# Projections: second and fourth output change places from group to group, and the narrow groups' weight sums go to VectorE

## The chip, the cores and the metric

The kernel runs on one core of one Trainium2 chip. A core has five engines that run side by side, each with its own queue of instructions, taken in order: TensorE (PE in the profile; its weight loads are PEld), VectorE (DVE), ScalarE (ACT), GpSimd (POOL) and SyncE (SP), which here issues the DMA transfers. They hand work to each other by semaphores. The metric is the time of one execution in microseconds (us), as the median of several runs.

## The reference

One decoder layer over 2048 tokens of width 1024, in float32: a normed input, one combined projection, two mixers (gated linear attention and dilated sliding-window attention), an output projection and an MLP. The change touches only the combined projection:

```python
nx = rmsnorm(h, attn_norm_g[l])
proj = jnp.einsum('bsd,dp->bsp', nx, w_in[l])
gq, gk, gv, gr, glow, dq, dk_, dv_ = jnp.split(proj, split_at, axis=-1)
```

`gq`, `gk` are 256 columns each, `gv`, `gr`, `dq`, `dk_`, `dv_` 512 each, and `glow`, the low-rank input of the forget gate, 16.

## The kernel before

The projection is a matrix product of tokens (2048 x 1024) by weights (1024 x columns). It is done in two halves of 1024 tokens, and the columns in nine groups (L169): `dv`, `gr`, `dq`, `dk`, `dq`, `dk`, `gq`, `gk`, `gv`. So there are 18 groups `g`. Six are wide (a pair of 256 or 264 columns), twelve are narrow (`dq`, `dk`, `gq`, `gk`: a pair of 128 columns).

Each group is a 2 x 2 block product: two blocks of 512 tokens, two halves of the 1024 inputs, two blocks of columns. It is done with seven block products instead of eight, by sums of blocks ahead of and behind the products. A group therefore runs the products in the order 1, 2, 5, 6, 3, 4, 7 (L173), one job each. TensorE computes each float32 product as three products of a high and a low part (`mm3`, L63 to L66). A narrow job is 12 matmuls of 512 columns: four chunks of 128 inputs, three matmuls each.

**Weights.** The four blocks a11, a12, a21, a22 of a group lie in two buffers (`wraw`). `prep` (L196) makes ready one job's weights: ACT copies the block, scaled, into a rounded high part (L206), and DVE subtracts to get the low part (L208; L210 where there is a scale). The results go to one of three buffers (`wcomb`), two jobs ahead of the product. Between the jobs, blocks are summed in place: at job 2 a21 += a22 (L213), at job 5 a21 -= a11 (L215) and a12 -= a21 (L217), at job 6 a21 = a22 - a21 (L219). L211 chooses the engine of these sums: DVE in a wide group, GpSimd in a narrow one. As soon as a block is no longer needed, the same block of the next group is loaded over it: a11 after the sum at job 5, a12 behind job 3, a22 behind job 4, a21 behind job 7 (L215 and the lines behind it; L189 is the transfer, on SP's queue). The next group's sum at job 2 needs that last load.

**Outputs.** `product` (L280) computes a job into one of four PSUM banks in turn (tags a, c, a, o), and its `rest` (L298) takes it into the output buffers. There are six of these in SBUF: X, c11, c12, c21, c22 and `last`. Product 1 is copied to X (ACT, L307); product 2 plus X is the first output (DVE, L309); product 5 is copied to the fourth (ACT, L312); product 6 is added to X (L314), and X plus the fourth gives the start of the second (L315, DVE); product 3 completes the second (L317); product 4 is copied to the third (L320); product 7 is added to X (L322), and X to the third and the fourth (L323, L324). First, second, third and fourth output are always c11, c12, c21 and c22.

**Stores.** `finish` (L240) stores an output when it is complete: the first after product 2, the second after product 3, the fourth and the third after product 7. In a `dq` or `dk` group ACT and DVE first split it into a high and a low part in place (L252, L253), and SP stores both (L254, to qD or kD). In a `gq` or `gk` group it is stored as it is (L248). A buffer can be written by the next group once its store has read it. In a `gr` group the output passes through a sigmoid on ACT and DVE (L127 to L130, L264, L265) and a product on GpSimd (L266), and the 16 columns of `glow` go to `gate` (L227 to L238), whose small matmuls (L232, L235) and copies (L230, L233) run among those of the next groups.

**Order.** The first pieces of work are ordered by hand. Then a loop over jobs emits `prep(at + 2)`, `product(at)` and, in some places, a step of other work: the second token half's norm (L95, L96, L424, L426), its transposes (L374) and their copies and sums (L430 to L439). The order in which each engine runs all that is set by a scheduler with its own estimate of times, so an edit can move instructions that it doesn't name.

Of the kernel before, what the change touches and what calls it, by code (L numbers as in the profile page):

```python
# [14 lines left out]
OP = mybir.AluOpType  # L15
# [23 lines left out]
def emit(tc, a, stop=99):  # L39
    nc = tc.nc  # L40
    V, A, G, T, SP = nc.vector, nc.scalar, nc.gpsimd, nc.tensor, nc.sync
# [6 lines left out]
    def ps(tag):  # L48
        return psum.tile([128, 512], F32, name="ps_" + tag, tag=tag, bufs=BANKS[tag])
# [5 lines left out]
    def view(t, shape):  # L55
        n = int(np.prod(shape))
        names = "abcd"[:len(shape)]
        return t[:, :n].rearrange(f"p ({' '.join(names)}) -> p {' '.join(names)}", **dict(zip(names, shape)))
# [9 lines left out]
    def token_rows(ap, c, row, width=D):  # L68

        return bass.AP(tensor=ap.tensor, offset=ap.offset + c * 128 * row,  # L70
                       ap=[[row, 16], [16 * row, 8], [1, width]])
# [54 lines left out]
    def log_sigmoid(e, p):  # L126
        A.activation(e, p, AF.Abs)  # L127
        A.activation(e, e, AF.Exp, scale=-1.0)
        A.activation(e, e, AF.Ln, bias=1.0)
        V.scalar_tensor_tensor(e, p, 0.0, e, op0=OP.min, op1=OP.subtract)  # L130
# [27 lines left out]
    GP = 1056  # L158
    xp, bp, acc = slot("xp"), slot("bp"), [slot("acc") for _ in range(3)]
    CX, c11, c12, c21, c22, last = [t[:, GP * q:GP * q + GP] for t in acc for q in range(2)]  # L160
    C = [[c11, c12], [c21, c22]]
    stg_ring = view(last, (4, 264))
    stg_at = [0]

    def stage():
        stg_at[0] = (stg_at[0] + 1) % 4
        return stg_ring[:, stg_at[0]]
# [17 lines left out]
    def load_w(g, n, k):  # L185

        if g < 2 * NG:
            _, c0, w = groups[g % NG]
            SP.dma_start(raws[n][:, k, :, :w], w_in[:, 4 * k:4 * k + 4, c0 + n * w:c0 + n * w + w])  # L189

    def comb(at, w):

        t = view(combs[at % 3], (2, 4, max(w, 256)))
        return [t[:, q, :, :w] for q in range(2)]

    def prep(at):  # L196

        if at >= len(jobs):
            return
        g, j = jobs[at]  # L200
        kind, _, w = groups[g % NG]
        (a11, a12), (a21, a22) = [[raws[n][:, k, :, :w] for k in range(2)] for n in range(2)]
        hi, lo = comb(at, w)
        src = {1: a11, 2: a12, 5: a21, 6: a21, 3: a12, 4: a22, 7: a21}[j]
        sc = scales.get(kind, 1.0)
        A.activation(hi, src, AF.Copy, scale=sc)  # L206
        if sc == 1.0:
            V.tensor_tensor(lo, src, hi.bitcast(F32), op=OP.subtract)  # L208
        else:
            V.scalar_tensor_tensor(lo, src, sc, hi.bitcast(F32), op0=OP.mult, op1=OP.subtract)  # L210
        Y = V if w > 128 else G  # L211
        if j == 2 and g:
            Y.tensor_tensor(a21, a21, a22, op=OP.add)  # L213
        if j == 5:
            Y.tensor_tensor(a21, a21, a11, op=OP.subtract)  # L215
            load_w(g + 1, 0, 0)
            Y.tensor_tensor(a12, a12, a21, op=OP.subtract)  # L217
        if j == 6:
            Y.tensor_tensor(a21, a22, a21, op=OP.subtract)  # L219
        if j == 3:  # L220
            load_w(g + 1, 0, 1)
        if j == 4:
            load_w(g + 1, 1, 1)
        if j == 7:
            load_w(g + 1, 1, 0)

    def gate(glow, t):  # L227

        gT = gTs[t % 2]
        V.memset(gT, 1.0)  # L230
        pt = ps("d")
        T.transpose(pt[:16, :128], glow, ident)  # L232
        V.tensor_copy(gT[:16], pt[:16, :128])  # L233
        pg = ps("d")[:, :256]
        T.matmul(pg, gT, w2b, start=True, stop=True)  # L235
        e = stage()[:, :256]
        log_sigmoid(e, pg)
        SP.dma_start(glD[t * 128:t * 128 + 128], e)  # L238

    def finish(g, n, k, i):  # L240

        kind, c0, w = groups[g % NG]
        tb = 2 * (g // NG) + k
        c = C[n][k]
        if w == 128:
            tk = slice(512 * tb, 512 * tb + 512)
            if kind in ("gq", "gk"):
                SP.dma_start((gqD if kind == "gq" else gkD)[n, :, tk], c[:, :512])  # L248
                return
            pr = (c0 - (DQ if kind == "dq" else DK)) // 128 + n  # L250
            hi = c[:, 512:1024].bitcast(FR)
            A.activation(hi, c[:, :512], AF.Copy)  # L252
            V.tensor_tensor(c[:, :512], c[:, :512], hi.bitcast(F32), op=OP.subtract)  # L253
            SP.dma_start((qD if kind == "dq" else kD)[pr][:, :, tk], view(c, (2, 512)))  # L254
            return
        t = 4 * tb + i
        tk = slice(t * 128, t * 128 + 128)
        s = c[:, i * w:i * w + w]
        if kind == "gr":
            j = n * w  # L260
            m = min(w, 512 - j)
            sg = stage()[:, :m]
            log_sigmoid(sg, s[:, :m])
            A.activation(sg, sg, AF.Exp)  # L264
            V.tensor_tensor(s[:, :m], sg, s[:, :m], op=OP.mult)  # L265
            G.tensor_tensor(s[:, :m], s[:, :m], gnB[:, j:j + m], op=OP.mult)  # L266
            SP.dma_start(srD[tk, j:j + m], s[:, :m])
            if m < w:
                gate(s[:, m:w], t)
            return  # L270
        j = n * w
        if kind == "dv":
            SP.dma_start(token_rows(vN[:, j:], t, 512, w), s)
        if i == 3:
            SP.dma_start((vD if kind == "dv" else gvD)[512 * tb:512 * tb + 512, j:j + w].rearrange("(i p) n -> p i n", i=4),
                         c[:, :4 * w].rearrange("p (i n) -> p i n", i=4))
# [3 lines left out]
    def product(at, i):  # L280

        g, j = jobs[at]
        kind, _, w = groups[g % NG]
        p = ps("acao"[banks[0] % 4])
        banks[0] += 1
        B, W = TB[j], comb(at, w)
        n = w
        if w == 128:
            n = 512
            for c in range(4):  # L290
                mm3(p, W[0][:, c], W[1][:, c], B[0][:, c], B[1][:, c], c == 0, c == 3)
        else:
            p = p[:, :w]
            tk = slice(i * 128, i * 128 + 128)
            for c in range(4):
                mm3(p, B[0][:, c, tk], B[1][:, c, tk], W[0][:, c], W[1][:, c], c == 0, c == 3)

        def rest():  # L298
            X, c11, c12, c21, c22 = [v[:, i * n:i * n + n] for v in (CX, *C[0], *C[1])]
            q = p  # L300
            if kind == "dq":
                q, ix, i11, i12, i21, i22 = [v.rearrange(f"p (c {o}) -> p c r i", c=4, i=8) for v, o in
                                             ((p, "r i"), *((v, "i r") for v in (X, c11, c12, c21, c22)))]
            else:
                ix, i11, i12, i21, i22 = X, c11, c12, c21, c22
            if j == 1:
                A.activation(ix, q, AF.Copy)  # L307
            elif j == 2:
                V.tensor_tensor(i11, q, ix, op=OP.add)  # L309
                finish(g, 0, 0, i)  # L310
            elif j == 5:
                A.activation(i22, q, AF.Copy)  # L312
            elif j == 6:
                V.tensor_tensor(ix, q, ix, op=OP.add)  # L314
                V.tensor_tensor(c12, X, c22, op=OP.add)  # L315
            elif j == 3:
                V.tensor_tensor(i12, q, i12, op=OP.add)  # L317
                finish(g, 0, 1, i)
            elif j == 4:
                A.activation(i21, q, AF.Copy)  # L320
            else:
                V.tensor_tensor(ix, q, ix, op=OP.add)  # L322
                V.tensor_tensor(c21, c21, X, op=OP.add)  # L323
                V.tensor_tensor(c22, c22, X, op=OP.add)  # L324
                finish(g, 1, 1, i)
                finish(g, 1, 0, i)

        return rest
# [28 lines left out]
    X = {}  # L357
# [120 lines left out]
    with tc.manual_schedule(engines={nc.tensor.engine, nc.vector.engine, nc.scalar.engine, nc.gpsimd.engine}):  # L478
# [45 lines left out]
        a21, a22 = [raws[1][:, k, :, :256] for k in range(2)]  # L524
# [16 lines left out]
        kept(3, pv3)  # L541
        x_scale(5)
        prep(2)
        x_stat(6)
        first_half(4, pv4)
# [36 lines left out]
    for at in range(5, len(jobs)):  # L582
        g = jobs[at][0]
# [720 lines left out]

    def output(C, half, t, i, last=False):

        scr = sums["scr"][:, 512 * (i % 4):512 * (i % 4) + 512]
        ss = stat(2)
        for n in range(2):
            A.activation(scr, C[n], AF.Square, accum_out=ss[:, n:n + 1])  # L1310
            if n == 0:
                G.tensor_tensor(C[0], C[0], gF[:, :512], op=OP.mult)  # L1312
        s1 = stat()
        V.tensor_tensor(s1, ss[:, 0:1], ss[:, 1:2], op=OP.add)
        r = rstd_of(s1, D)
        V.scalar_tensor_tensor(C[1], C[1], r, gF[:, 512:], op0=OP.mult, op1=OP.mult)
        A.activation(C[0], C[0], AF.Copy, scale=r)
# [68 lines left out]
    for at in range(7, len(jobs1)):  # L1386
# [13 lines left out]
        if at in (len(jobs1) - 4, len(jobs1) - 2):  # L1400
            n = (at + 4 - len(jobs1)) // 2
# [5 lines left out]
    for ph, (j, half) in enumerate(phases):  # L1407
        P = [bank() for _ in range(4)]
        for k in range(8):
            n = 8 * ph + k  # L1410
# [74 lines left out]
```

## Time and profile before

| what | value |
|---|---|
| median of 3 runs | 2330.84 us (2328.76 to 2331.72) |
| the profiled execution | 2328.52 us |
| its span, first to last instruction | 2326.7 us |
| mean granted clock of TensorE | 0.995 of full speed |
| TensorE busy | 2286.6 us, 98% of the span |
| VectorE busy | 1571.9 us, 68% |
| ScalarE busy | 1146.3 us, 49% |
| GpSimd busy | 434.9 us, 19% |

In the rows of the profile a line such as L213 is a line of the kernel before. A row of a timeline has the start in us, the duration, the engine, the line, the operation, the tiles (output <- inputs), the shape, and in brackets how long the engine sat idle before and what ended that. A row of groups has the count, the busy time, the mean of one in ns, and the idle time before them with what ended it. The projections fill about the first 520 us of the span.

### The profile page before, as it was taken

How to read it: one execution, taken by the hardware profiler on the slowest of the kernel's cores; microseconds unless marked ns; L12 is line 12 of the kernel's file. 1: busy time of each engine (PE TensorE's matmuls, PEld its weight loads, DVE VectorE, ACT ScalarE, POOL GpSimd, SP SyncE). 2: the span in 40 equal slices, each digit the busy share in tenths (PEclk: the TensorE clock that was granted, in tenths of full speed). 3: DMA queues.
4: the chain of work that ended last, by engine and by line, in shares of the span. 5: the costliest groups of instructions: out<-in, count | busy, mean ns of one | idle time of the engine just before them, and what ended most of it. 6: DMA issues, size and time to landing. Idle time of an engine off the chain costs nothing.

```text
span 2326.7 us, 34991 instructions
## 1 busy us (share of the span) xinstructions
PE 2286.6 (98%) x12652; PEld 1974.4 (85%) x12652; DVE 1571.9 (68%) x2926; ACT 1146.3 (49%) x2200; POOL 434.9 (19%) x530
## 2 busy tenths in 40 slices
PE   8999999999999999999999999999999999999998
PEld 7977998789999998888888887888888888888886
DVE  8878778766676786446877788777765446447445
ACT  6565446535676773224555566555544323224324
POOL 1133103235387785000000000000000100001002
PEclk9999999999999999999999999999999999999999
DMA  4547754777666964778644447444486477447543
GB/s 158 152 153 246 227 178 123 214 226 244 196 218 209 296 194 158 221 233 269 209 155 152 157 155 261 165 150 150 149 276 236 162 271 262 139 160 270 202 162 109
DMA packets 341804, 457.59 MB, mean 197 GB/s; under 512 B 18117, under 2 KB 214230, under 8 KB 336256
## 3 DMA queue, kind: packets, MB, share of 16 engines
q1 hardware_dynamic: 336878, 446.71, 59.2%
q10 hardware_dynamic: 4754, 8.66, 1.0%
q8 instruction: 99, 1.62, 0.3%
q14 instruction: 73, 0.60, 0.1%
HBM read 292.99 MB, written 167.02 MB: 198 GB/s over the span
## 4 chain that ended last, share of the span: by engine, by line
PE 48%; DVE 2%; DMA 2%; issue 1%; ACT 0%; POOL 0%; POOLq 0%; DVEq 0%; ACTq 0%
PE ps_c L65 6%; PE ps_c L64 6%; PE ps_c L66 6%; PE ps_a L65 4%; PE ps_a L66 4%; PE ps_a L64 4%; PE ps_d L64 4%; PE ps_d L65 4%; PE ps_d L66 4%; PE ps_o L65 2%; PE ps_o L64 2%; PE ps_o L66 2%; DMA rb<-w_ff 1%; DMA rb<-hTD 0%; DVE cb L352 0%
## 5 line engine op out<-in xcount | busy, mean ns | idle before, releaser
L352 DVE TENSOR_TENSOR ca<-ra,ca 128x1024 fp32r<-128x1024 f32 x112 | 137.7, 1230 | 162.0 <-ACT ca L351 162.0
L1312 POOL TENSOR_TENSOR suma<-suma,gs 128x512 f32<-128x512 f32 x16 | 23.3, 1470 | 1146.6 <-ACT scr L1310 1146.5
L351 ACT ACTIVATE ca<-ra 128x1024 fp32r<-128x1024 f32 x112 | 117.9, 1053 | 223.6 <-PE ps_c L66 178.6
L351 ACT ACTIVATE w1comb<-w1raw 128x512 fp32r<-128x512 f32 x224 | 139.9, 627 | 155.3 <-PE ps_c L66 58.1
L352 DVE TENSOR_TENSOR w1comb<-w1raw,w1comb 128x512 fp32r<-128x512 f32 x224 | 154.0, 689 | 52.4 <-ACT w1comb L351 52.2
L716 ACT ACTIVATE pe<-pe,O 128x256 f32<-128x256 f32 (+1 forms) x384 | 155.7, 454 | 61.0 <-DVE O L715 59.0
L744 PE MATMUL ps_a<-v,pt 128*128 128x65 f32 x1200 | 178.3, 252 | 0.9 <-DVE pt L734 0.5
L744 PEld LDWEIGHTS ps_a<-v,pt 128*128 128x128 f32 x1200 | 175.3, 194 | 2.7 <-DVE pt L734 0.7
L725 PE MATMUL ps_d<-ident,pe 128*128 128x128 f32 x600 | 157.5, 278 | 3.2 <-ACT pt L732 3.0
L715 DVE CUSTOM_DVE_ANT_0 pe<-ps_c,nb 128x256 f32<-128x256 f32 (+1 forms) x384 | 125.8, 361 | 34.9 <-PE ps_d L725 15.9
L206 ACT ACTIVATE wcomb<-wraw 128x512 fp32r<-128x512 f32 (+2 forms) x126 | 96.6, 774 | 93.4 <-PE ps_o L65 22.2
L351 ACT ACTIVATE cb<-rb 128x1024 fp32r<-128x1024 f32 x56 | 59.4, 1061 | 162.1 <-PE ps_o L65 104.3
L65 PE MATMUL ps_c<-hb,w1comb 128*128 128x512 f32 x336 | 130.9, 390 | 0.6 <-DVE w1comb L352 0.6
L66 PE MATMUL ps_c<-hb,w1comb 128*128 128x512 f32 x336 | 130.8, 389 | 0.0
L64 PE MATMUL ps_c<-hb,w1comb 128*128 128x512 f32 x336 | 130.7, 389 | 0.0
L66 PE MATMUL ps_c<-cb,ca 128*128 128x512 f32 x336 | 130.7, 389 | 0.0
L64 PE MATMUL ps_c<-cb,ca 128*128 128x512 f32 x336 | 130.7, 389 | 0.0
L65 PE MATMUL ps_c<-cb,ca 128*128 128x512 f32 x336 | 130.7, 389 | 0.0
L725 PEld LDWEIGHTS ps_d<-ident,pe 128*128 128x128 f32 x600 | 107.7, 184 | 3.8 <-ACT pt L732 3.2
L208 DVE TENSOR_TENSOR wcomb<-wraw,wcomb 128x512 fp32r<-128x512 f32 (+2 forms) x84 | 89.8, 1070 | 28.8 <-ACT wcomb L206 28.2
L352 DVE TENSOR_TENSOR cb<-rb,cb 128x1024 fp32r<-128x1024 f32 x56 | 68.2, 1222 | 59.8 <-ACT cb L351 59.7
L1178 ACT ACTIVATE acc<-acc 128x512 f32<-128x512 f32 x128 | 79.6, 631 | 47.9 <-DVE acc L1198 35.9
(402 smaller groups left out, 7150.5 us busy)
## 6 DMA issues: line engine op xcount, KB each, us to landing
ra<-actD SPq DMA_DIRECT2D x56, 1024.0 KB, 6.9
actD<-acc SPq DMA_DIRECT2D x192, 256.0 KB, 2.4
rb<-w_ff SPq DMA_DIRECT2D x72, 512.0 KB, 4.5
w1raw<-w_ff SPq DMA_DIRECT2D x32, 1024.0 KB, 5.8
k<-kD SPq DMA_DIRECT2D x16, 1024.0 KB, 8.5
rb<-hTD SPq DMA_DIRECT2D x13, 1024.0 KB, 6.1
wraw<-w_in SPq DMA_DIRECT2D x48, 256.0 KB, 4.3
cmb<-boD SPq DMA_DIRECT2D x16, 528.0 KB, 6.4
```

Of the source, the lines that this page charges most:

```text
L64: T.matmul(out, sh, mh, start=first, stop=False)
L65: T.matmul(out, sl, mh, start=False, stop=False)
L66: T.matmul(out, sh, ml, start=False, stop=last)
L206: A.activation(hi, src, AF.Copy, scale=sc)
L208: V.tensor_tensor(lo, src, hi.bitcast(F32), op=OP.subtract)
L351: A.activation(hi, src, AF.Copy)
L352: V.tensor_tensor(lo, src, hi.bitcast(F32), op=OP.subtract)
L715: V.tensor_tensor_reduce(p, s, bias, scale=1.0, scalar=BIG, op0=OP.add, op1=OP.min, accum_out=nm)
L716: A.activation(p, p, AF.Exp, bias=nm, scale=-1.0)
L725: T.transpose(pb[:, i * 128:i * 128 + 128], src, ident)
L744: T.matmul(self.b.opsum[:, n % 4], self.pt[:, i * 128:i * 128 + 128], self.b.v[:, blk, cols], start=first, stop=last)
L1178: A.activation(v, v, AF.Relu)
```

## The change

Two edits. The first gives the second output and the fourth output of a group c12 and c22 by turns: in an even group as before, in an odd group the second is c22 and the fourth c12. So product 5's copy writes the buffer that held the previous group's second output, not its fourth. The second edit takes the choice of engine away: the sums of weights run on VectorE in the narrow groups too, 48 sums of 128 x 512. As the scheduler works anew, the order of instructions on all engines differs between about 103 and 300 us and again between about 370 and 490 us; elsewhere it is the same. The number of matmuls is the same.

```diff
-    C = [[c11, c12], [c21, c22]]
...
-        Y = V if w > 128 else G
         if j == 2 and g:
-            Y.tensor_tensor(a21, a21, a22, op=OP.add)
+            V.tensor_tensor(a21, a21, a22, op=OP.add)
         if j == 5:
-            Y.tensor_tensor(a21, a21, a11, op=OP.subtract)
+            V.tensor_tensor(a21, a21, a11, op=OP.subtract)
             load_w(g + 1, 0, 0)
-            Y.tensor_tensor(a12, a12, a21, op=OP.subtract)
+            V.tensor_tensor(a12, a12, a21, op=OP.subtract)
         if j == 6:
-            Y.tensor_tensor(a21, a22, a21, op=OP.subtract)
+            V.tensor_tensor(a21, a22, a21, op=OP.subtract)
...
+    def outputs(g):
+
+        return (c11, (c12, c22)[g % 2], c21, (c22, c12)[g % 2])
+
     def finish(g, n, k, i):
...
-        c = C[n][k]
+        c = outputs(g)[2 * n + k]
...
-            X, c11, c12, c21, c22 = [v[:, i * n:i * n + n] for v in (CX, *C[0], *C[1])]
+            X, c11, c12, c21, c22 = [v[:, i * n:i * n + n] for v in (CX, *outputs(g))]
```

## The prediction

> **What bounds the kernel now.** I read the page's busy table first, then the windows of 20 us, then TensorE's timeline where a window falls short of 20.
>
> ```profile
> PE 2286.6 (98%) x12652; PEld 1974.4 (85%) x12652; DVE 1571.9 (68%) x2926; ACT 1146.3 (49%) x2200; POOL 434.9 (19%) x530
> ```
>
> TensorE is the bound: 98% of the span. A change that keeps its 12,652 matmuls, as this one does, can only win where TensorE idles or is throttled. The rewritten lines run in two places, the narrow groups of the first token half (about 103 to 300 us) and of the second (370 to 490 us).
>
> ```profile
> 100.00:200.00 100.00, 94.19 (x465) 75.05 (x464) 81.56 (x138) 62.54 (x139) 38.05 (x30) 0.98 0.59 181
> ...
> 400.00:500.00 100.00, 98.89 (x429) 78.02 (x427) 71.78 (x103) 45.90 (x84) 30.75 (x21) 1.00 0.72 209
> ...
> 160.00:180.00 20.00, 17.58 (x73) 12.64 (x72) 14.10 (x25) 12.83 (x27) 5.29 (x4) 0.91 0.46 148
> ```
>
> Columns: the stretch, its length, busy time of PE, PEld, DVE, ACT, POOL, then the granted clock. TensorE lacks 5.8 and 1.1 us, and in 160 to 180 the clock is 0.91, worth 20 x 0.09 = 1.8 us. Part of the first 5.8 lies before 138 us and between matmuls; the stalls within reach are these:
>
> ```profile
> 156.38 0.39 PE L66 MATMUL ps_a<-tb,wcomb 128*128 128x512 f32 x1
> 158.22 0.69 PE L235 MATMUL ps_d<-misc 17*128 17x256 f32 x2 [1.45 <-DVE misc L233]
> 159.63 0.50 PE L64 MATMUL ps_a<-tb,wcomb 128*128 128x512 f32 x1 [0.72 <-ACT wcomb L206]
> 160.50 0.50 PE L65 MATMUL ps_a<-tb,wcomb 128*128 128x512 f32 x1 [0.37 <-DVE wcomb L210]
> ...
> 162.28 0.63 PE L65 MATMUL ps_a<-tb,wcomb 128*128 128x512 f32 x1
> ...
> 179.61 0.47 PE L64 MATMUL ps_o<-tb,wcomb 128*128 128x512 f32 x1 [1.84 <-DVE acc L309]
> ...
> 200.08 0.66 PE L374 MATMUL ps_d<-perm,xp 128*128 128x128 f32 x4 [1.30 <-DVE stats L95]
> ...
> 201.34 0.50 PE L65 MATMUL ps_a<-tb,wcomb 128*128 128x512 f32 x1 [0.36 <-DVE wcomb L208]
> ...
> 243.01 0.50 PE L65 MATMUL ps_a<-tb,wcomb 128*128 128x512 f32 x1 [0.74 <-DVE wcomb L208]
> ...
> 421.62 0.50 PE L64 MATMUL ps_o<-tb,wcomb 128*128 128x512 f32 x1 [0.93 <-ACT acc L312]
> ```
>
> Around 158: 1.45 + 0.72 + 0.37 = 2.54, then the slow clock (0.63 instead of 0.39 us a matmul). With 1.84, 1.66, 0.74 and 0.93 the stalls are 7.7 us, with the clock 9.5: the most that can be won.
>
> **Part 1, the outputs change places.** ACT's copy into the fourth output (L312, product 5) must wait until the previous group's last store out of that buffer is read.
>
> ```profile
> 156.34 0.60 ACT L312 ACTIVATE acc<-ps_c 128x512 f32<-128x512 f32 x1 [5.15 <-DMA qD<-acc]
> ```
> ```profile
>   DMA qD<-acc: 13.1, 3
>   DMA kD<-acc: 13.1, 4
> ...
>   DMA gkD<-acc: 4.5, 1
> ```
>
> L312 sat 30.7 us over both halves, on ACT, and TensorE feels it only at 158 (the chain L312, L315, L230, L233, L235) and 421.6. After the swap it writes the buffer of the previous second output, whose store comes from product 3 instead of 7; L315, one product later, takes over the write onto the fourth.
>
> At 158 (third to fourth narrow group of the first half) the rows are:
>
> ```profile
> 142.57 0.68 DVE L324 TENSOR_TENSOR acc<-acc 128x512 f32<-128x512 f32 x1
> ...
> 152.00 0.67 DVE L208 TENSOR_TENSOR wcomb<-wraw,wcomb 128x512 fp32r<-128x512 f32 x1
> ...
> 163.77 1.27 DVE L426 SCALAR_TENSOR_TENSOR xp<-xp,stats,misc 128x1024 f32<-128x1024 f32 x1
> ```
> ```profile
> 150.90 0.52 SPq L254 DMA_DIRECT2D qD<-acc  x1
> 151.53 1.90 SPq L189 DMA_DIRECT2D wraw<-w_in  x2
> ```
> ```profile
> 158.47 1.42 POOL L213 TENSOR_TENSOR wraw<-wraw 128x512 f32<-128x512 f32 x1 [9.88 <-DMA wraw<-w_in]
> ```
>
> In the changed program's order both previous stores stand soon after L324 and two sums, so I put their issue at 146 to 147; before, the awaited one took 5.4 us (150.90 to 156.34), so L312 starts at 150 to 152. But product 7's split (L206) now stands behind L312 in ACT's queue. The split's low half, last reader of a21, ends at 152.5 to 153.9 (152.67 before), and SP can only then issue the load that refills it. With 3.9 to 5 us for that load it lands at 156.4 to 158.8 (158.47 before). The next group's first sum waits for it, now on DVE, and behind it stand L95, L426 (1.27) and L210: L426 ends at 158.3 to 160.7, while TensorE wants it at 156.6 + 0.7 = 157.3, then L210. The stall is 1.3 to 4.0, middle 2.3, in place of 2.54 + 1.8: **-2.0** (-3.2 to +1.5, the latter if the clock drops again). The Trainium skill, "TensorE: Matmul & The Clock Gate", Part 1, has the clock halve after one idle window of about 3.4 us; the rows show the drop after 2.54 us of idle spread over 4 us and none after 1.84, so the trace doesn't bear the figure out; by the page the 1.8 us would have another cause and stay, and the sum below would be -2.7.
>
> At 421.6 L312 would start near 417 instead of 420.97: **-1.0** (-1.1 to 0; 0 if the earlier store lands no sooner).
>
> **Part 2, 48 sums move from POOL to DVE.**
>
> ```profile
> L215 POOL TENSOR_TENSOR wraw<-wraw 128x512 f32<-128x512 f32 x12 | 20.7, 1722 | 30.2 <-DVE wcomb L210 19.1 <-DVE wcomb L208 11.1
> L213 POOL TENSOR_TENSOR wraw<-wraw 128x512 f32<-128x512 f32 x12 | 17.9, 1492 | 103.8 <-DMA wraw<-w_in 84.9 <-DVE acc L130 10.0 <-DMA nTD<-bp 9.0
> ...
> L217 POOL TENSOR_TENSOR wraw<-wraw 128x512 f32<-128x512 f32 x12 | 17.3, 1440 | 0.9
> L219 POOL TENSOR_TENSOR wraw<-wraw 128x512 f32<-128x512 f32 x12 | 17.1, 1426 | 12.3 <-DVE wcomb L210 6.7 <-DVE wcomb L208 4.2 <-DVE misc L230 1.4
> ```
>
> POOL loses 73.0 us. DVE has the same shape of work in L323, so it gains 48 x 0.68 = 33 us, and an undisturbed sum is 0.8 us shorter. What DVE gets back is in its own rows between 140 and 240 us:
>
> ```profile
> L208 DVE TENSOR_TENSOR wcomb<-wraw,wcomb 128x512 fp32r<-128x512 f32 x16 | 13.7, 857 | 2.6 <-ACT wcomb L206 2.3
> L253 DVE TENSOR_TENSOR acc<-acc 128x512 f32<-128x512 f32 x14 | 12.5, 902 | 0.5 <-ACT acc L252 0.4
> L210 DVE SCALAR_TENSOR_TENSOR wcomb<-wraw,wcomb 128x512 fp32r<-128x512 f32 x14 | 11.3, 823 | 3.9 <-ACT wcomb L206 3.9
> L426 DVE SCALAR_TENSOR_TENSOR xp<-xp,stats,misc 128x1024 f32<-128x1024 f32 x6 | 8.7, 1450 | 2.9 <-POOL stats L96 2.9
> L324 DVE TENSOR_TENSOR acc<-acc 128x512 f32<-128x512 f32 x5 | 5.6, 1121 | 0.0
> L323 DVE TENSOR_TENSOR acc<-acc 128x512 f32<-128x512 f32 x5 | 3.4, 683 | 0.1
> ```
>
> L324 and L323 are the same operation and shape, yet 1121 and 683 ns: L324 runs while POOL sums. Against 0.68 (L426: the 1.27 above) the excess is 16 x 0.18 + 14 x 0.22 + 14 x 0.14 + 6 x 0.18 + 5 x 0.44 = 11.2 us. The 17 sums of that stretch (POOL's rows there are 5, 4, 4 and 4) cost DVE 17 x 0.68 = 11.6. DVE's load stays nearly as it is, and instructions get back to even lengths:
>
> ```profile
> 175.41 3.13 DVE L253 TENSOR_TENSOR acc<-acc 128x512 f32<-128x512 f32 x2
> ...
> 197.72 2.31 DVE L426 SCALAR_TENSOR_TENSOR xp<-xp,stats,misc 128x1024 f32<-128x1024 f32 x1 [0.44 <-POOL stats L96]
> ```
>
> The stall at 179.61 is L309 behind two L253 at 3.13 where 1.36 would do; the order on TensorE also puts product 7 of the group before first: **-1.7** (-1.84 to -0.5, if the two sums that now stand ahead of L309 take the relief). At 200 and 201, L426 falls by 1.04 and its L96 no longer queues behind sums on POOL, but L213, L215 and L217 stand ahead on DVE: **-0.7** (-1.66 to 0). The 0.74 at 243 I leave at **0** (-0.7 to 0).
>
> What DVE's order costs: L213 waits for its load with the rest of DVE's queue behind it; on POOL only L96 and L266 stood there. Fourth to fifth group: L317 of product 3 frees the bank that TensorE takes for the next group's product 2, and in the changed order it stands behind L213, L438 and L439. Counted from product 6's last matmul: the low half of product 7 ends after some 1.4 (L314, L210), a load of 4.5 lands at 5.9, and four instructions of 0.68 end at 8.6 (7.5 with a load of 3.4, 9.7 with 5.6). TensorE is there after products 3, 4 and 7, 36 matmuls 0.227 apart (138.62 to 140.90 below are ten steps), and 0.3 for the next product's first: 8.5. I take **+0.5**, from 0 to +5.4 (a load of 8 us would make it 3.6, with 1.8 of clock). Second to third group: the low half L208 comes behind L213, whose load landed at 138.03:
>
> ```profile
> 138.03 1.86 POOL L213 TENSOR_TENSOR wraw<-wraw 128x512 f32<-128x512 f32 x1 [2.05 <-DMA wraw<-w_in]
> ```
> ```profile
> 138.62 0.39 PE L65 MATMUL ps_o<-tb,wcomb 128*128 128x512 f32 x1
> ...
> 140.90 0.39 PE L66 MATMUL ps_o<-tb,wcomb 128*128 128x512 f32 x1
> ```
>
> It then ends at 138.03 + 0.68 + 0.68 = 139.4, where TensorE's first matmul with it began at 138.62: 0.8 late if the load lands as before, nothing if it is issued a little sooner. Half of it, **+0.4** (0 to +1.3), for this and its like in the second half. The other groups have 1 to 4 us between L213 and the first wanted result in the changed order: 0, as long as loads take their usual time. The load after L215 is issued about 1 us sooner, which nobody awaits.
>
> **Sum:** -2.0 - 1.0 - 1.7 - 0.7 + 0.5 + 0.4 = -4.5 us. The profiled execution, 2328.52, becomes 2324.0; it stands 2.3 below the median, so the median 2330.84 becomes **2326.3**. Ends: all best -8.5 (2322.3), all worst +7.7 (2338.5). After 520 us the order is unchanged and TensorE is full, so a gain passes on.
>
> **Rivals.**
>
> *DVE's in-order wait becomes the bound (slower).* Place: L213 in the 12 narrow groups. For it: its wait on POOL was 84.9 us. Against it: DVE is idle 18% of 100 to 200 us and 28% of 400 to 500, and most groups have slack.
>
> ```profile
> DMA to landing us min/median/max: 2.8/4.7/9.5
> ```
>
> Loads spread from 2.8 to 9.5 us, more than the slack. It decides where the 12 pass on 5.4 / 12 = 0.45 us each on average (5.4: the four gains). At 1 us each, an estimate from that spread, it is +12 - 5.4 = +6.6: 2337.4.
>
> *All stalls go.* If the stores land at once and the fourth group's load comes at 156.4, TensorE gets 8.5 to 9.5 back: 2322. Against it: L213 and the split stand in the queues that feed it.
>
> *The stalls only change names.* L312's wait passes to the held-back second store, L426 to the sums ahead; the four gains vanish, +0.5 and +0.4 stay: 2331.7. The Trainium skill, "Perfetto Trace Analysis", says that offloading between GpSimd and DVE "might not help", since they share a read port; the neutral load (11.2 against 11.6) agrees with it, the shorter sums are what it doesn't count.
>
> **How the numbers follow.** Chances: forecast (-2.5 to -7) 0.46, all stalls go 0.12, only names 0.14, the wait on DVE 0.28. About 0.2% (4.7 us) is what a measurement of this kernel tells from no change. The forecast straddles it, 0.30 beyond and 0.16 within: faster 0.30 + 0.12 = 0.42, same 0.16 + 0.14 = 0.30, slower 0.28. The range, 2321 to 2338, goes from all stalls gone to nearly the worst sum; the forecast's own is 2324 to 2328.5.
>
> **What the profile after would show.** No sum left on POOL; 48 rows of 128x512 on DVE at 0.68; L324 and L253 near 0.68, L426 near 1.27. L312's waits on qD, kD and gkD well below 30.7 in all. TensorE's stalls near 179 and 421 gone, near 158 about 2.3 and without 0.63 us matmuls behind it. Wrong if DVE's L213 waits for its load for several us and TensorE then waits for L208, L210, L317 or L426; or if the clock falls below 1 in another window.

## The result and the profile after

The changed kernel takes 2322.58 us, the median of six runs (2319.07 to 2323.48), beside 2331.3 us before (2328.76 to 2334.73): 8.7 us less. The ratio is 0.9956, with a 95% interval of 0.9946 to 0.9966. The forecast was 2326.3 in a range of 2321 to 2338: the right way and inside the range, but the gain is almost twice the 4.5 us expected, and the rival "all stalls go" (2322) is nearest.

First the busy table of the page after, which answers to the first lines shown of before.

```profile
PE 2288.0 (99%) x12652; PEld 1977.1 (85%) x12652; DVE 1567.8 (68%) x2974; ACT 1147.0 (49%) x2200; POOL 368.4 (16%) x482
```

GpSimd (POOL) has 48 instructions and 66.5 us less (the sums took 73.0, but the product L266, here L268, takes 38.2 us where it took 31.6), VectorE (DVE) 48 instructions more, and yet VectorE is 4.1 us less busy than before (1571.9). The windows after, with the columns of the prediction:

```profile
100.00:200.00 100.00, 97.14 (x487) 77.49 (x486) 84.52 (x161) 65.58 (x144) 20.37 (x16) 0.99 0.62 189
200.00:300.00 100.00, 100.00 (x644) 91.06 (x643) 78.39 (x115) 48.23 (x75) 1.48 (x2) 0.99 0.77 237
...
400.00:500.00 100.00, 100.00 (x444) 80.42 (x443) 74.06 (x122) 45.54 (x81) 0.42 (x1) 1.00 0.75 226
```

TensorE lacks 2.9 us between 100 and 200 where it lacked 5.8, and nothing in 400 to 500 where it lacked 1.1. All its stalls of 0.3 us or more between 100 and 500 us are in these rows of its timeline (the lines of `prep` stand one or two lower here, so L206 is L205, L208 is L207 and L213 is L211; those behind the new function two higher, so L317 is L319):

```profile
186.35 0.50 PE L64 MATMUL ps_a<-tb,wcomb 128*128 128x512 f32 x1 [1.06 <-DVE acc L319]
...
196.48 0.51 PE L64 MATMUL ps_a<-tb,wcomb 128*128 128x512 f32 x1 [1.24 <-ACT wcomb L205]
197.41 0.50 PE L65 MATMUL ps_a<-tb,wcomb 128*128 128x512 f32 x1 [0.42 <-DVE wcomb L207]
...
198.54 0.63 PE L66 MATMUL ps_a<-tb,wcomb 128*128 128x512 f32 x1
...
201.10 0.63 PE L66 MATMUL ps_a<-tb,wcomb 128*128 128x512 f32 x1
```

The stalls of before at 158, 179, 243 and 421 us are gone. New is 1.06 at 186; the one near 200 is as long as it was (1.24 + 0.42 = 1.66, before 1.30 + 0.36). Behind it the clock falls: the matmuls from 198.54 to 201.10 are 0.43 apart instead of 0.227, which is 8 x 0.2 = 1.6 us (the clock is 0.96 in the windows of 180 to 200 and of 200 to 220 us). So 2.7 of stall and 1.6 of clock are left of 7.7 and 1.8: 5.2 us gone.

The spans differ by 5.5 (2326.7 to 2321.2), less than the medians' 8.7. Where the difference lies is seen from two matmuls that both kernels have: the first of `gate`'s transposes (L232, here L230) and the first matmul behind the projections (L703, here L705). TensorE's timeline before, then after:

```profile
115.98 0.27 PE L232 MATMUL ps_d<-ident,acc 128*16 128x128 f32 x1
...
544.16 0.30 PE L703 MATMUL ps_c<-k,qp 128*128 128x256 f32 x1
```
```profile
116.98 0.27 PE L230 MATMUL ps_d<-ident,acc 128*16 128x128 f32 x1
...
538.50 0.30 PE L705 MATMUL ps_c<-k,qp 128*128 128x256 f32 x1
```

Between the two lie 428.2 us before and 421.5 after: the changed stretch is 6.7 us shorter; 5.2 of them are the stalls and the clock above, where the other 1.5 lie is not shown. This execution came 1.0 us later to that stretch, and behind it the two are alike (1782.5 and 1782.7 us to the end of the span). The rest of the medians' 8.7 is which execution was profiled: the one of before (2328.52) is below all six timed runs of its kernel, and the one after (2323.05) is 0.5 above its median.

VectorE's groups between 140 and 240 us after, which answer to groups shown of before; the last row is one of the moved sums:

```profile
L207 DVE TENSOR_TENSOR wcomb<-wraw,wcomb 128x512 fp32r<-128x512 f32 x18 | 12.8, 710 | 3.5 <-ACT wcomb L205 3.5
L255 DVE TENSOR_TENSOR acc<-acc 128x512 f32<-128x512 f32 x15 | 10.2, 682 | 0.4 <-ACT acc L254 0.4
L209 DVE SCALAR_TENSOR_TENSOR wcomb<-wraw,wcomb 128x512 fp32r<-128x512 f32 x14 | 9.5, 679 | 2.5 <-ACT wcomb L205 2.4
L428 DVE SCALAR_TENSOR_TENSOR xp<-xp,stats,misc 128x1024 f32<-128x1024 f32 x6 | 7.7, 1277 | 0.0
...
L326 DVE TENSOR_TENSOR acc<-acc 128x512 f32<-128x512 f32 x5 | 3.4, 682 | 0.0
...
L211 DVE TENSOR_TENSOR wraw<-wraw 128x512 f32<-128x512 f32 x4 | 2.8, 693 | 2.9 <-DMA wraw<-w_in 2.9
```

The mean of the last sum of an output fell from 1121 to 682 ns, of the splits of outputs from 902 to 682, of the norm's product from 1450 to 1277. ACT's wait for a store in front of product 5's copy, 30.7 us over both halves before, is 4.9 in all (each row has the us and the number of waits):

```profile
  DMA qD<-acc: 3.8, 2
...
  DMA gkD<-acc: 1.1, 1
```

### The profile page after: what moved, and what is told of

Same layout as the page of the kernel before. It is cut to its first block, busy times and chain, and to the rows that moved or that the text cites. A ratio compares the mean times of both kernels' runs of the same rounds, so it can differ in the third digit from the quotient of the medians.

```text
span 2321.2 us, 34949 instructions
## 1 busy us (share of the span) xinstructions
PE 2288.0 (99%) x12652; PEld 1977.1 (85%) x12652; DVE 1567.8 (68%) x2974; ACT 1147.0 (49%) x2200; POOL 368.4 (16%) x482
## 3 DMA queue, kind: packets, MB, share of 16 engines
q8 instruction: 99, 1.62, 0.3%
## 4 chain that ended last, share of the span: by engine, by line
PE 48%; DVE 2%; DMA 2%; issue 1%; ACT 0%; POOL 0%; POOLq 0%; DVEq 0%; ACTq 0%
PE ps_c L65 6%; PE ps_c L64 6%; PE ps_c L66 6%; PE ps_a L65 4%; PE ps_a L66 4%; PE ps_a L64 4%; PE ps_d L64 4%; PE ps_d L66 4%; PE ps_d L65 4%; PE ps_o L65 2%; PE ps_o L64 2%; PE ps_o L66 2%; DMA rb<-w_ff 1%; DMA rb<-hTD 0%; DVE cb L354 0%
## 5 line engine op out<-in xcount | busy, mean ns | idle before, releaser
L205 ACT ACTIVATE wcomb<-wraw 128x512 fp32r<-128x512 f32 (+2 forms) x126 | 97.2, 774 | 91.0 <-issue 22.7
L96 POOL TENSOR_TENSOR stats<-stats,mhalf 128x1 f32<-128x1 f32 (+1 forms) x64 | 49.6, 779 | 348.1 <-DVE stats L95 348.1
```

The costliest lines, as they stand in the source:

```text
L96: G.tensor_tensor(r2, r, mhalf[:, :n], op=OP.pow)
```

## The experiments

Each kernel is measured beside the kernel before, so the figure of before differs a little from place to place; the ratio is that of the two, with its 95% interval. The theory at the start: two separate effects, shorter waits for stores by the outputs' exchange and shorter VectorE instructions by the sums' move. The rivals: one of the two does all of it; the order that the scheduler finds does it; the sums' own way is shorter. The diffs stand against the kernel before or the changed one, and all these kernels keep the line numbers of the kernel before.

### The exchange alone

Against the kernel before: only `outputs(g)`, the sums stay on GpSimd.

> Outputs change places, sums stay on GpSimd. Theory (two separate effects): the waits of ACT's L312 on the stores fall, so the stalls at 158 and 421 us (2.54, the slow clock behind it 1.8, and 0.93) shrink by 3 to 4 us in all, while DVE stays slowed beside GpSimd (L324 and L253 over 0.8 us) and the stalls near 179 and 200 (1.84, 1.66) stay: 2327 to 2329, 2 to 4 us below before. Rival (the new order of instructions wins, not the buffers): no gain by itself, 2330 to 2333, with L312's waits much shorter all the same.

Measured: 2332.27 us against 2331.96 before, ratio 0.9997 (0.9988 to 1.0005). No gain. TensorE's timeline, where the exchange should have helped:

```profile
160.44 0.69 PE L235 MATMUL ps_d<-misc 17*128 17x256 f32 x2 [1.19 <-DVE misc L233]
161.85 0.50 PE L64 MATMUL ps_a<-tb,wcomb 128*128 128x512 f32 x1 [0.72 <-ACT wcomb L206]
...
423.87 0.50 PE L64 MATMUL ps_o<-tb,wcomb 128*128 128x512 f32 x1 [1.77 <-ACT acc L312]
```

Neither of the two stalls that the exchange was to shorten has gone; the one behind L312 is longer (0.93 before). Near 181 us, 0.95 and 0.92 us stand for the 1.84 of before, and the clock is 0.91 in 160 to 180 and in 180 to 200 us. The rows behind the stall at 160, from ACT's and SP's timelines:

```profile
158.55 0.60 ACT L312 ACTIVATE acc<-ps_c 128x512 f32<-128x512 f32 x1 [4.89 <-DMA qD<-acc]
```
```profile
153.11 0.52 SPq L254 DMA_DIRECT2D qD<-acc  x1
```

L312 waits 4.89 us where it waited 5.15. The second output is complete two products earlier than the fourth, but its split stands in VectorE's queue behind the same late instructions as the fourth's, so the store that is now awaited is issued at 153.11 and lands 5.4 us later, as the other did. My theory's half on the exchange falls.

### The sums alone

Against the kernel before: the line that chooses the engine gives VectorE always.

> All weight sums on VectorE, outputs as before. Theory (two separate effects): L324, L253 and L426 fall to 0.68, 0.68 and 1.27 us and the stalls near 179 and 200 shrink by 2 to 3.5 us, L312 still waits about 30 us on stores and TensorE still stalls near 158 and 421: 2327 to 2329. Rival (one cause, both stalls come from a late DVE): DVE's shorter instructions alone take away nearly all, 2322 to 2324, as in the changed kernel.

Measured: 2325.41 us against 2331.96, ratio 0.9966 (0.9953 to 0.9979): most of the gain, and between the two expected ranges. In its trace the largest stall from 100 to 500 us is 1.13 us:

```profile
163.82 0.66 PE L374 MATMUL ps_c<-perm,xp 128*128 128x128 f32 x4 [1.13 <-DVE xp L426]
```

and there is none near 421, although L312 still waits for stores, 32.8 us in all:

```profile
  DMA kD<-acc: 16.6, 4
  DMA qD<-acc: 8.2, 4
...
  DMA gkD<-acc: 4.6, 1
  DMA srD<-acc: 3.4, 2
```

So those waits are not what TensorE felt. At the place of the long stall L312 starts at 153.89 here; it was 156.34 before, and it is 150.50 in the changed kernel (there L314). First this kernel's ACT timeline, then the changed one's:

```profile
153.89 0.60 ACT L312 ACTIVATE acc<-ps_c 128x512 f32<-128x512 f32 x1 [2.89 <-DMA qD<-acc]
```
```profile
150.50 0.60 ACT L314 ACTIVATE acc<-ps_c 128x512 f32<-128x512 f32 x1 [0.77 <-DMA qD<-acc]
```

The first 2.5 us come without the exchange, and they are enough: no stall of `gate`'s matmul or of the product behind it is left there. What the exchange adds on top, 0.9956 and, run again, 0.9967 (below) against 0.9966, can't be told from nothing.

### Sums that nobody reads

Is it contention with GpSimd, or the sums' own shorter way? The changed kernel gets the load of GpSimd back without its dependences: 24 sums in all, four in each of the six narrow groups of the first half. One of them, in the first narrow group, writes into the part of X that the `gr` group ahead still needs, so a part of the gate output is not the reference's.

```diff
+    idle_sum = lambda g, s: g < NG and s.shape[-1] == 128 and G.tensor_tensor(view(CX[:, 512:], (4, 128)), s, s, op=OP.add)
...
             Y.tensor_tensor(a21, a21, a22, op=OP.add); idle_sum(g, a21)
```

> The changed kernel, plus 16 sums on GpSimd in each kind of the first token half's narrow groups that nobody reads (24 in all: the block just summed on VectorE, doubled into an unused part of X). If contention with GpSimd is what the change takes away: L324, L253 and L426 in 140 to 240 us grow again by some 10 us in all, now on top of VectorE's own 11.6 us of sums, TensorE stalls again by 5 us or more in 140 to 205: 2327 to 2332. If it is the shorter way of the sums themselves (0.68 instead of 1.4 us, and no queue on GpSimd), these extra sums hold up nobody: 2321 to 2324 as the changed kernel, with VectorE's rows hardly longer.

Measured: 2329.49 us against 2331.3, ratio 0.9992 (0.9984 to 1.0001): the whole gain is lost, with nothing taken from VectorE's work. In its trace the clock is 0.83 in 160 to 180 and 0.91 in 200 to 220 us, which is worth 5.2 us. To be sure that the one write into X wasn't the cause, the next kernel leaves it out.

> As the 24 idle sums, without the one in the first narrow group that wrote into X while the gr group still needed it: 23 sums on GpSimd that nobody reads, the result is the same. Contention: 2327 to 2331, TensorE stalls of 3 us or more in 140 to 205 with VectorE's two-input instructions over 0.75 us there. If the earlier run was slow because of that one write: 2321 to 2324.

Measured: 2327.43 us against 2333.25, ratio 0.9983 (0.9973 to 0.9992). The changed kernel stands at 0.9956 and, run again, at 0.9967, so 23 sums in one half only cost about 4 to 6 us, about half of the gain or more. TensorE's timeline and VectorE's groups from 140 to 240 us:

```profile
150.95 0.50 PE L65 MATMUL ps_a<-tb,wcomb 128*128 128x512 f32 x1 [1.10 <-DVE wcomb L208]
...
163.20 0.66 PE L374 MATMUL ps_c<-perm,xp 128*128 128x128 f32 x4 [1.86 <-DVE xp L426]
164.65 0.50 PE L65 MATMUL ps_a<-tb,wcomb 128*128 128x512 f32 x1 [0.79 <-DVE wcomb L210]
...
200.34 1.12 PE L374 MATMUL ps_d<-perm,xp 128*128 128x128 f32 x4 [2.34 <-DVE xp L426]
```
```profile
L210 DVE SCALAR_TENSOR_TENSOR wcomb<-wraw,wcomb 128x512 fp32r<-128x512 f32 x14 | 12.7, 919 | 0.0
L253 DVE TENSOR_TENSOR acc<-acc 128x512 f32<-128x512 f32 x15 | 11.9, 792 | 0.7 <-ACT acc L252 0.7
```

6.1 us of stalls, each behind a VectorE instruction, with means of 919 and 792 ns where the changed kernel has 679 and 682; behind the last of them the clock is 0.91 (1.8 us). The first of these stalls, at 150.95, stands where TensorE, ACT and VectorE still run in the changed kernel's order; on TensorE the orders part only in a stretch of the first half, from about 165 us. This is shown: GpSimd's sums cost time by slowing VectorE, though nobody reads them. A rest stays open: an idle sum also holds its blocks until it is done (VectorE waited 2.29 and 0.33 us for one, ACT 2.76 and a load 0.9), so not all of the loss need be contention. What the scheduler's new order gives by itself in the changed kernel was not separated.

### Copies in place of the idle sums

The same 23 places, with one input.

```diff
-    ... G.tensor_tensor(view(CX[:, 512:], (4, 128)), s, s, op=OP.add)
+    ... G.tensor_copy(view(CX[:, 512:], (4, 128)), s)
```

> The changed kernel plus 23 GpSimd copies of 128x512 (one input in SBUF, not two) in the first token half, each of a block just summed, into an unused part of X; the result is the same. If any GpSimd read of SBUF slows VectorE's two-input instructions, the time goes back to 2327 to 2331, as with the idle sums, and L208, L210 and L253 are again 0.1 us or more above 0.68 in 140 to 240 us. If it needs two inputs on GpSimd, or if the idle sums only held up the blocks that they read, it stays at 2321 to 2324 with VectorE's rows at 0.68.

Measured: 2321.29 us, ratio 0.9959 (0.9946 to 0.9971): no loss, 6.1 us below the sums beside it, and the two intervals don't touch. The order is not the cause of these 6.1 us: up to about 190 us TensorE, ACT and VectorE have the same order in both kernels, and there the sums made 3.75 us of stalls, the copies 1.62. But VectorE is not untouched, so neither expectation holds whole:

```profile
L210 DVE SCALAR_TENSOR_TENSOR wcomb<-wraw,wcomb 128x512 fp32r<-128x512 f32 x14 | 11.1, 806 | 0.0
L253 DVE TENSOR_TENSOR acc<-acc 128x512 f32<-128x512 f32 x15 | 10.8, 723 | 0.9 <-ACT acc L252 0.9
```

The excess is about a half and a third of that of the sums (127 and 41 ns against 240 and 110), and a copy is shorter: 1027 ns in the mean against 1548 of a sum. One stall of 1.62 us came of it, with the clock at 0.92 behind it, where the sums made 6.1. It seems that VectorE has some slack and that the copies stay nearly inside it; that was not tested further.

### Which half

Sums of the first half on GpSimd again, of the second on VectorE.

```diff
-        Y = V
+        Y = V if w > 128 or g >= NG else G
```

> Outputs change places everywhere; sums of the first token half's narrow groups on GpSimd as before, those of the second half on VectorE. If the gain lies where VectorE is crowded by the second half's norm and transposes (the first token half), little is left: 2329 to 2332, with the stalls of 158 to 205 us back, and 420 to 440 us full. If both halves gain by the move: 2325 to 2328.

Measured: 2328.34 us against 2331.3, ratio 0.9987 (0.9978 to 0.9996). So about 3 us come from the second half and the rest from the first; the time lies just between the two expected ranges. The stalls of 158 to 203 us are back (4.4 us, with the clock at 0.91 in 160 to 180 and in 180 to 200), none is left near 421. That the first half weighs more because the norm and the transposes of the second token half crowd VectorE there fits, but was not tested.

### The first sum, off VectorE or later

The cost that I had put on VectorE's in-order wait for the load, by two kernels. One puts only the first sum of a narrow group (L213) back on GpSimd; the other holds it behind the low half of product 2.

```diff
-            Y.tensor_tensor(a21, a21, a22, op=OP.add)
+            (V if w > 128 else G).tensor_tensor(a21, a21, a22, op=OP.add)
```

> The changed kernel, but the first sum of each narrow group (L213, which waits for the load) back on GpSimd; the other 36 sums on VectorE. Theory (DVE's in-order wait in L213 costs TensorE 1.06 us near 186 and little elsewhere): that stall goes, about 1 us below the changed kernel: 2321 to 2322, L213's 22 us of DVE wait gone. Rival (contention with GpSimd decides): 12 sums beside DVE's two-input instructions slow it again by about 8 us in all, some of it reaches TensorE: 2324 to 2326.

```diff
+            (tc.keep_in_program_order if w == 128 else id)(Y.tensor_tensor(a21, a21, a22, op=OP.add))
```

> The changed kernel, but the first sum of each narrow group is held on VectorE behind the low half of product 2 (L208 or L210), about one product later in DVE's queue, so what TensorE wants next no longer stands behind the wait for the load. Theory: the stall near 186 (1.06) goes and the wait for loads in L213 falls from 22 us to under 8: 1 to 2 us below the changed kernel, 2320.5 to 2321.5. Rival (a late sum makes the later product's split late, or the order that the scheduler then finds is worse elsewhere): 2323 to 2328, with a new wait of L206 on L213.

Measured: 2322.77 us, ratio 0.9954 (0.9937 to 0.9971), and 2323.25 us, ratio 0.9962 (0.9948 to 0.9975). In both the stall at 186 is gone, as the theory said. But in the first the one near 196 has grown to 1.23 + 0.96, and in the second there are 0.95 and 0.52 near 178, with the clock at 0.96 in 160 to 200. No gain can be told. The wait is real and its price is about a microsecond, and the next order of the scheduler loses about as much elsewhere.

### The norm step one job later

In the changed kernel ACT waits for loads of x in front of the split that TensorE needs at 196 us. One number in the list of places for the other work moves that step.

```diff
-OTHER = ... for n in (0, 6, 10, 11, 12, 13)]
+OTHER = ... for n in (0, 7, 10, 11, 12, 13)]
```

> The changed kernel with the step of the second token half's norm (L424, L95, L426) one job later in each group pair, so that its loads have landed when ACT reaches it and L206 no longer stands behind an ACT that waits for them. Theory (in the changed kernel the stall of 1.24 and 0.42 at 196 us and the slow clock behind it come from that wait): 2 to 3 us below the changed kernel, 2319 to 2321, no stall near 196. Rival (the order that comes out is late elsewhere, since transposes and their stores then come later): 2322 to 2327 with another stall.

> The norm step one job later, the same program again: its first median was 2320.7, 1.9 us below the changed kernel beside it. If that is real, it stays below 2322 with one stall near 198 and none near 186; if it was scatter, 2322 to 2324.

Measured: 2320.72 us (0.9953, 0.9941 to 0.9966) and 2321.79 us (0.9958, 0.9943 to 0.9972). One stall is left, 2.19 us in the first trace and 3.19 in the second, at the same place:

```profile
198.56 0.50 PE L64 MATMUL ps_a<-tb,wcomb 128*128 128x512 f32 x1 [2.19 <-ACT wcomb L206]
```

The stall did not go away, and none is left at 186 and 197. ACT's rows of the first trace show why: the edit moved the loads of x along with the step (issued from 189.94 us, in the changed kernel from 187.54), so ACT waits for them as before, and longer.

```profile
193.42 1.06 ACT L424 ACTIVATE bp<-xp 128x1024 f32<-128x1024 f32 x1 [1.27 <-DMA xp<-x]
...
196.36 1.06 ACT L424 ACTIVATE bp<-xp 128x1024 f32<-128x1024 f32 x1 [1.27 <-DMA xp<-x]
```

The two waits together are 1.14 us in the changed kernel run again (below), 1.70 in its first trace, 2.54 here and 3.55 in the second trace here; TensorE's stall behind them is 0.94, 1.66, 2.19 and 3.19. These four agree with the theory of the wait for x; the edit did not remove that wait. Both medians are below the changed kernel's two (2322.58 and 2322.61), by 0.8 to 1.9 us, and the intervals overlap: whether it beats the changed kernel is open. The step together with the held first sum:

> The changed kernel with the norm step one job later and the first sum of each narrow group held behind the low half of product 2. If the stall near 198 (2.19 before L206) stood behind waits in VectorE's queue: it shrinks to under 1, 2318 to 2320. If the scheduler's new order trades it for others, as the held sum alone did: 2321 to 2324.

Measured: 2325.04 us, ratio 0.9972 (0.9961 to 0.9983). A stall of 4.12 us at 205, with the clock at 0.91 from 200 to 220, and two small ones (0.77 and 0.43). ACT waits 5.22 + 0.46 us for the loads of x, which are issued only at 194.87 and 196.28. The median is above that of either move alone and 1 us above the second expectation's range, though the intervals overlap.

### The changed kernel again

> The changed kernel itself once more, its statements written on the lines of the kernel before, same instructions in the same order on every engine. If the stalls and the clock's dips differ from run to run and only their mean counts, its median is again 2321 to 2324 with single runs 4 to 5 us apart, while the profile shows the same stalls near 186 and 196 with or without a slow clock behind them.

Measured: 2322.61 us, ratio 0.9967 (0.9954 to 0.9979). The stall at 186 is there to the tenth (1.12), the one at 196 is shorter and the clock stays at 1.00 behind it:

```profile
186.36 0.50 PE L64 MATMUL ps_a<-tb,wcomb 128*128 128x512 f32 x1 [1.12 <-DVE acc L317]
...
195.94 0.49 PE L64 MATMUL ps_a<-tb,wcomb 128*128 128x512 f32 x1 [0.51 <-ACT wcomb L206]
196.87 0.50 PE L65 MATMUL ps_a<-tb,wcomb 128*128 128x512 f32 x1 [0.43 <-DVE wcomb L208]
```

In these two traces the stall behind an order is the same; the one behind a transfer and the clock's dip are not. But much of the scatter lies where nothing was changed: over the fourteen traces the first of `gate`'s transposes comes between 115.98 and 119.25 us, and from L703 to the end it takes 1780.0 to 1786.6. That is why one profile isn't enough to weigh 2 us. The stretch between the two is the better measure of a single trace, and it ranks the kernels much as the medians do: before 428.2, the exchange alone 428.0, 24 idle sums 427.3, 23 idle sums 425.4, the first half on GpSimd 424.9, the sums alone 422.0, the changed kernel 421.5 and again 419.5, idle copies 419.0.

## Why the prediction was right and wrong

**Bound and places.** Right: TensorE's stalls between 138 and 243 us and at 421 were what there was to win, and 5.2 of 9.5 us went in the profiled pair. That the forecast's 4.5 is near this is partly luck, since its terms missed both ways. In the order of the sum, with 243 and the new dip of the clock behind them, the pair gives -4.34 - 0.93 - 1.84 + 0 + 1.06 + 0 - 0.74 + 1.6 = -5.2. The forecast's 4.5 is about half of the medians' 8.7. And one of my signs of being wrong did appear in this trace, though not in the other: the clock fell in another window.

**Part 1, -2.0 at 158.** The size was too small and the reason wrong. The measured change there is the whole 4.3. I had L312 start at 150 to 152 because of the exchange, and it did (150.50), but the exchange alone left it at 158.55, and the sums alone removed that stall with L312 at 153.89. What made the difference is the VectorE queue ahead of the store, which I had put into the sum only at 179 and 200. And I had TensorE arrive at 157.3: it reached the transposes (L374 before, L376 here) only at 158.99, with no idle time, while their input was ready at 158.93 (157.66 + 1.27). About 1.1 us of that delay is this execution's late start; for the rest, one of `gate`'s transposes and a first matmul of the next product stand ahead. VectorE's and TensorE's timelines after:

```profile
156.99 0.69 DVE L211 TENSOR_TENSOR wraw<-wraw 128x512 f32<-128x512 f32 x1 [0.92 <-DMA wraw<-w_in]
...
157.66 1.27 DVE L428 SCALAR_TENSOR_TENSOR xp<-xp,stats,misc 128x1024 f32<-128x1024 f32 x1
```
```profile
158.99 0.66 PE L376 MATMUL ps_c<-perm,xp 128*128 128x128 f32 x4
```

The load that the first sum awaits had landed by 156.99. That is inside my 156.4 to 158.8, but without the late start it is 155.9, sooner than my earliest: the low half of product 7 ended at 153.87, and the load took 3.1 us from there, where I had allowed 3.9 to 5. So the term most mis-sized is the stall of 2.3 us that I left there: it was nothing. The clock's 1.8 went, as forecast.

**Part 1, -1.0 at 421.** The stall went (0.93), but again not by the exchange, which alone made it 1.77.

**Part 2, VectorE's load neutral.** Right: busy 1571.9 before, 1567.8 after, with 48 sums of 0.68 us more. The lengths came out as said (0.68, 0.68, 1.28). What I drew from it was too little: "neutral" is the sum over the queue, while single instructions that TensorE waits for come sooner (L426 took 2.31 us at 197.72 and takes 1.27 at 197.27), and this was credited at two places instead of along every chain.

**-1.7 at 179** came true to a tenth (1.84). **-0.7 at 200** did not: 1.66 as before in one trace, 0.94 in the other, once with 1.6 of slow clock; L426 did fall to 1.27, and a wait of ACT for loads of x (in its L424, here L426) took its place, behind which the split stands that TensorE wants:

```profile
193.76 1.06 ACT L426 ACTIVATE bp<-xp 128x1024 f32<-128x1024 f32 x1 [1.15 <-DMA xp<-x]
```

**0 at 243** was 0.74.

**What VectorE's order costs.** The fourth to fifth group came as worked out, at L317 behind L213 and its followers: 1.06 and 1.12 us against +0.5 (0 to +5.4). The first sum's wait on VectorE is 22.4 us in all, and this is the one place where a stall of TensorE follows from it in these traces. The +0.4 at the second to third group was nothing.

**The rivals.** The slower one (VectorE's wait passes on in all 12 groups) needed 0.45 us each; 1.1 us came in all. "All stalls go" has the nearest time (2322), but in the trace not all went: 2.7 of stall and 1.6 of clock are left, in the second trace 2.1 and no dip. "Only the names change" describes the exchange alone. The Trainium skill, "Perfetto Trace Analysis", section "Optimizing Scalar/DVE Operations", says that offloading between these two engines might not help, since they share a read port. Here the move from GpSimd to VectorE does help, by 0.34% (the sums alone). That the two slow each other agrees with the page's reason, though no run shows the port itself; in this kernel the sum on GpSimd costs VectorE about as much as doing it (11.2 against 11.6 us), and takes twice as long (1.52 us in the mean, against 0.68).

## What to carry to other kernels

As this kernel shows, elementwise work on GpSimd with two inputs in SBUF (the on-chip memory) need not be free help to a busy VectorE: compare the same shape on VectorE inside and outside the stretches where GpSimd runs, and if the excess is about the length of the sums, move them. When a wait for a buffer is shortened, first ask whether its release is late for a reason that stays: here the store was late because its split stood in a slow queue, and another buffer's split stood in the same queue. And where a scheduler orders everything anew, judge by medians of several runs and by doing one part alone, since a stall of a microsecond can move without leaving; and when a step is moved later to give its loads time, check that the loads don't move with it.

## What the runs showed of the hardware

**In these rows the two engines take turns by whole instructions.** With the 23 idle sums, GpSimd's and VectorE's timelines from 147 us (the second row is the second of the first row's two sums, seen alone):

```profile
147.35 2.99 POOL L163 TENSOR_TENSOR acc<-wraw 128x512 f32<-128x512 f32 x2 [3.46 <-DVE wraw L215]
148.98 1.37 POOL L163 TENSOR_TENSOR acc<-wraw 128x512 f32<-128x512 f32 x1
```
```profile
147.31 0.69 DVE L217 TENSOR_TENSOR wraw<-wraw 128x512 f32<-128x512 f32 x1
147.91 1.53 DVE L253 TENSOR_TENSOR acc<-acc 128x512 f32<-128x512 f32 x1
149.41 0.17 DVE L230 MEMSET misc<- 17x128 f32 x1
149.51 1.38 DVE L208 TENSOR_TENSOR wcomb<-wraw,wcomb 128x512 fp32r<-128x512 f32 x1
```

The first sum is over by 148.98, the second at 150.35. L217, which began just ahead of the first sum, keeps its 0.69 us; the sum takes 1.6, where the shortest of the 23 takes 1.03. L253 ends at 149.44, 0.46 behind the first sum, and L208 at 150.89, 0.54 behind the second: each as if it had worked only once the sum was over (alone it takes 0.68). The Trainium skill, "SBUF — State Buffer", section "SBUF: two separate sides", says that a VectorE operation with two SBUF inputs and a GpSimd operation that reads SBUF exclude each other for a whole instruction. These rows agree with it. With the copies, which have one input, VectorE's instructions lengthen too (L210 806 ns in the mean against 679).

**The clock falls after stalls of very different length, and not always.** Idle of 1.47 us (first sum later), 1.62 (idle copies) and 1.66 (after) was followed by a dip; 1.84 (before, at 179), 2.19 (norm step) and 2.65 (23 idle sums, at 163) were not; 2.34, 2.54, 3.19 and 4.12 were. The windows of 160 to 180 us, of the idle copies and of the 23 idle sums, show one dip and none:

```profile
160.00:180.00 20.00, 20.00 (x87) 15.32 (x87) 16.14 (x29) 11.71 (x24) 4.93 (x5) 0.92 0.54 168
```
```profile
160.00:180.00 20.00, 17.35 (x80) 12.79 (x81) 16.03 (x28) 12.15 (x26) 7.70 (x4) 1.00 0.51 170
```

Such a dip costs 1.6 to 1.8 us (20 us times what the clock lacks), about as much as a stall; with the 24 idle sums the window of 160 to 180 us lost 3.4. No threshold can be read from these; whether it is a matter of where the stall falls was not tested. The Trainium skill, "TensorE: Matmul & The Clock Gate", Part 1, has windows of about 3.4 us that run freely, and the clock halved after an idle one. By that a stall's place would decide, which fits the mixed cases, but the dips behind 1.47 to 2.54 us of idle came without a whole idle window.
